# Channel-major products of a split-precision transformer block: a weight part times both halves of the input in one matmul

## The chip, the cores and the metric

The kernel runs on one core of a Trainium2 chip. The metric is the time of one execution on the device in microseconds (us), as the median over runs.

## What is computed

The reference takes 256 tokens of width 2048 through two blocks, in float32. The first has a mixer (a two-way state-space scan beside pooling), a gated convolutional network of width 5632 and a gated embedding. The second has attention with forgetting (16 heads of 128) and retention (8 heads). Nearly all of the work is in products of the 256 x 2048 activations, or wider ones, with large weight matrices:

```python
proj = hn @ w_in[i]                      # 2048 -> D_IN_PROJ, mixer
mix = concatenate([y_ssd, y_pool]) @ w_out[i]
up = hn @ w_up                           # 2048 -> 2 * 5632
... (gelu(conv(gate)) * val) @ w_down    # 5632 -> 2048
proj = einsum('bsd,de->bse', x, w_in)    # attention, retention
```

## The kernel before, in words

**Precision by parts.** Weights w and activations x are each held as a sum of two float32r parts, a high and a low one. A product is taken as `hi(w)*hi(x) + hi(w)*lo(x) + lo(w)*hi(x)`, so three matmuls stand for one.

**The stream of weights.** `Stream` (lines 84 to 172) loads pieces of 512 rows x 512 columns (1 MB) in the order of their use, up to four raw pieces ahead. `_split` (lines 105 to 125) makes the two parts of a piece: ScalarE (ACT) copies to `hi` (line 122), VectorE (DVE) subtracts to `lo` (line 123). `pump` (line 148) issues loads and splits when there are free slots; it is called at the start of each piece through `get` (line 162), and with `most=1` around the end of a unit. All engines run their instructions in the order in which the program gives them.

**Two kinds of units.** Each produces 512 output columns. `unit_a` (line 280) is token-major: two accumulators of 128 tokens x 512 columns (`pa`), activations as the stationary operand, 512 weight columns moving. `unit_b` (line 325) is channel-major: the weights are stationary, and the output has channels on the partitions and 256 tokens along the free axis (`pb`). It has four blocks j of 128 channels, two in each accumulator of [128, 2, 256], so two accumulators in all. Per k-tile q and block j it issues three matmuls of 256 columns (lines 339 to 341). There are 39 such units of 4 pieces with 4 k-tiles each: 6 in the mixer (B and C, x twice, the pooling input u, z twice), 21 in the gated network (a value and a gate unit in turn, the first value unit being token-major), 4 gates of attention, 8 query/key units of retention. That makes 39 x 4 x 4 x 4 = 2496 triples.

**Accumulators.** All PSUM tiles come from one pool with eight buffers of one bank each (line 180), whatever their use: `pa`, `pb`, and the small products of the work in between. A new tile takes a bank that is free; its first matmul waits until the former tile of that bank has been read for the last time.

**Work in between.** At the end of each piece `tick` (line 250) runs what `defer` put off, then the next `fillers`: the scan of the mixer by a hand-written list (`SCHED`, line 26), and the heads of attention. At a unit's end `unit_b` calls `pump(1)`, hands the first accumulator to the caller's function `evac(0, ...)`, ticks, and defers the second to the first tick of the next unit (lines 345 to 349). What `evac` does depends on the caller: the convolution of five taps in the mixer (`conv5`, line 623), pooling sums (`f_u`, line 645), the convolution of three taps, gelu and the product with the value (`eg`, line 975), silu times the attention output (line 1224), rotation (line 1278). The value units of the gated network keep their accumulators as they are until the gate unit after them has ended (lines 968 to 971).

**Temporaries.** Tiles of 512 floats per partition come from a pool of eight (`temp`, line 194). The transposed activations `xt[i]` are [128, 2, 4, 256]: part, k-tile, token (line 382).

Of the kernel before, what the change touches and what calls it, by code (L numbers as in the profile page):

```python
# [12 lines left out]
AF = mybir.ActivationFunctionType  # L13
# [3 lines left out]
P = 128  # L17
S = 256
D = 2048
# [3 lines left out]
MAXPAIR = 7  # L23
# (step of the state-space mixer, the weight piece after which it is put): D dt, B C B^T, A decays, X inputs, S masks,
# T states, Y outputs, G gates, Q sums of squares, N norms; the number is the pair of heads or the group
SCHED = [
# [6 lines left out]
OUT_ORDER = ((2, 0), (3, 0), (2, 1), (3, 1), (0, 0), (0, 1), (1, 0), (1, 1), (2, 2), (3, 2), (0, 2), (1, 2))  # L33
# the slots held by all but the weights while a piece is used: (how many pieces, slots)
LIVE = [
# [17 lines left out]
def constants():  # L53
    """Tables that depend on shapes alone."""
    i = np.arange(P)
    c1 = np.zeros((P, 1664), np.float32)
    c1[:, 0:128] = i[:, None] <= i[None, :]
    c1[:, 128:256] = i[:, None] >= i[None, :]
    c1[:, 256:384] = i[:, None] > i[None, :]
    c1[:, 384:512] = i[:, None] < i[None, :]  # L60
    c1[:, 512:640] = 1.0
    t = np.arange(S)
    for g, k in enumerate((2, 4, 8, 16)):
        cnt = np.clip(t + k - k // 2, 0, S) - np.clip(t - k // 2, 0, S)
        c1[:, 640 + g * S : 640 + (g + 1) * S] = np.float32(1.0) / cnt.astype(np.float32)
    ident = np.eye(P, dtype=np.float32)
    sel = np.zeros((P, 16), np.float32)
    for b in (0, 32, 64, 96):
        for h in range(16):
            sel[b + h, h] = 1.0  # L70
    mask = np.where(i[None, :] > i[:, None], np.float32(-1e30), np.float32(0.0)).astype(np.float32)
    c0 = np.concatenate([ident, mask, sel], axis=1)
    inv = np.float32(10000.0) ** (-np.arange(0, 256, 2, dtype=np.float32) / np.float32(256.0))
    ang = (np.arange(S, dtype=np.float32)[None, :] * inv.astype(np.float32)[:, None]).astype(np.float32)
    cs, sn = np.cos(ang), np.sin(ang)
    rope = np.concatenate([cs, cs, sn, sn], axis=1).astype(np.float32)
    lg = np.log1p(-np.exp2(-5.0 - np.arange(8, dtype=np.float64)))
    diff = t[None, :] - i[:, None]
    dec = np.where(diff[None] >= 0, np.exp(np.maximum(diff, 0)[None] * lg[:, None, None]) / 16.0, 0.0)
    decay = np.transpose(dec, (1, 0, 2)).reshape(P, 8 * S).astype(np.float32)  # L80
    return {"c_base": c0.astype(np.float32), "c_ssd": c1, "c_rope": rope, "c_decay": decay}


class Stream:
    """Weights in the order of their use: loaded ahead, each split in two float32r parts."""

# [40 lines left out]
    def fits(self, pairs, raws):  # L127
        """pairs, raws: how many are held; piece ndone is the first of the pairs"""
        d = self.ndone
        for t in range(d, d + max(pairs, 1) + 1):  # L130
            if self.live[t] + 2 * max(d + pairs - t, 0) + raws + (0 if t < d + pairs else 2) > NSLOT:
                return False
        return True

    def split_fine(self):
        """the first piece, k-tile by k-tile: yields after each"""
        key, parts, kt, n = self.order[0]
        r = self.raw.pop(0)
        hi = self.k.slot([P, kt, n], F32R, "hi")
        lo = self.k.slot([P, kt, n], F32R, "lo")  # L140
        self.pair[0] = (hi, lo)
        self.nsplit += 1
        for q in range(kt):
            self.k.nc.scalar.activation(hi[:, q], r[:, q], AF.Copy)
            self.k.nc.vector.tensor_sub(lo[:, q], r[:, q], hi[:, q].bitcast(F32))
            yield
# [28 lines left out]
class Kern:  # L175
# [9 lines left out]

# [1 line left out]
    def nm(self, s):  # L187
# [17 lines left out]

# [1 line left out]
    def mm(self, o, l, r, start, stop):  # L207
# [12 lines left out]
    def rstd(self, o, ssum, scale, eps):  # L220
        """1/sqrt(scale * ssum + eps)"""
        self.act(o, ssum, AF.Sqrt, scale=scale, bias=eps)
        self.nc.vector.reciprocal(o, o)
# [17 lines left out]

# [1 line left out]
    def fillers(self, fs, pieces):  # L243
# [20 lines left out]

# [1 line left out]
    def part_a(self, ps, toks, hi, lo, xs, n, first, last, mid=None):  # L266
        """token-major: ps[t] [128 tokens, n] += x^T' w"""
        kt = len(xs)
        for t in toks:
            o = ps[t][:, :n]  # L270
            c = slice(t * P, (t + 1) * P)
            for q in range(kt):
                self.mm(o, xs[q][0][:, c], hi[:, q, :n], first and q == 0, False)
                self.mm(o, xs[q][0][:, c], lo[:, q, :n], False, False)
            if mid:
                mid()
            for q in range(kt):
                self.mm(o, xs[q][1][:, c], hi[:, q, :n], False, last and q == kt - 1)

    def unit_a(self, keys, x, evac, n=512, phased=0, between=None, mid=None):  # L280
        """keys: the pieces; x(i): the k-tiles of piece i; the last `phased` pieces go token tile by token tile,
        with `between` between the two and `mid` shortly before the second's end"""
        W = self.W
        ps = [self.ps([P, 512], "pa") for _ in range(2)]
# [39 lines left out]
    def unit_b(self, keys, x, evac, nt=4):  # L324
        """channel-major: banks [128 channels, 2, 256 tokens] += w' x^T"""
        W = self.W
        ps = [self.ps([P, 2, S], "pb") for _ in range((nt + 1) // 2)]
        m = len(keys)
        for i in range(m):
            hi, lo = W.get(keys[i])  # L330
            xs = x(i)
            for q in range(len(xs)):
                xh, xl = xs[q]
                for j in range(nt):
                    o = ps[j // 2][:, j % 2]
                    c = slice(j * P, (j + 1) * P)
                    f = i == 0 and q == 0
                    e = i == m - 1 and q == len(xs) - 1
                    self.mm(o, hi[:, q, c], xh, f and j % 2 == 0, False)
                    self.mm(o, hi[:, q, c], xl, False, False)  # L340
                    self.mm(o, lo[:, q, c], xh, False, e)
            W.done()
            if i < m - 1:
                self.tick()
        W.pump(1)
        evac(0, ps[0])
        self.tick()
        self.defer(1, lambda: evac(1, ps[1]))
        W.pump(1)

    def rows_b(self, key, x, m):
        """few columns: [2 * 32, 256]: the high part's rows at 0, the low part's at 32"""
        W = self.W
        p = self.ps([P, 512], "pr")
        w, _ = W.get(key)
        for q in range(16):
            xh, xl = x(q // 4)[q % 4]
            self.mm(p[: 32 + m, :S], w[:, q, : 32 + m], xh, q == 0, False)
            self.mm(p[: 32 + m, :S], w[:, q, : 32 + m], xl, False, q == 15)
# [5 lines left out]

# [1 line left out]
    def new_t(self, name):  # L367
        return [None] * 4

    def xk(self, xt):  # L370
        return lambda i: [(xt[i][:, 0, q], xt[i][:, 1, q]) for q in range(4)]

    def to_t(self, src, xt, t, step=None):
        """the transpose of one token tile [128, 2048], in two parts"""
        for i in range(4):
# [16 lines left out]
    def evac_rms(self, y, ssq, g, u, t, p):  # L392
        """y = p * g and the sum of p squared"""
        c = slice(u * 512, (u + 1) * 512)
# [4 lines left out]
    def rms_add(self, h, y, ssq, t):  # L399
        """h += y * rstd, with the sums of squares of the new h"""  # L400
        r = self.tiny([P, 1], "r")
# [9 lines left out]
    def rms_apply(self, y, h, s2, g, t):  # L411
        """y = h * rstd * g"""
        r = self.tiny([P, 1], "r")
# [23 lines left out]

# [1 line left out]
    def plan(self):  # L439
# [75 lines left out]

# [1 line left out]
    def setup(self):  # L517
# [103 lines left out]

# [1 line left out]
    def conv5(self, dst, p, i0):  # L623
        """dst [128, 2, 256]: centred convolution of a bank p [128, 2, 256], then silu"""
        for j in range(2):
# [314 lines left out]

# [1 line left out]
    def ffn(self):  # L942
# [80 lines left out]

# [1 line left out]
    def ple(self):  # L1025
# [40 lines left out]

# [1 line left out]
    def fox(self):  # L1068
# [185 lines left out]

# [1 line left out]
    def ret(self):  # L1256
# [153 lines left out]
```

## Time and profile before

| | |
|---|---|
| runs | 2443.69, 2444.24, 2445.71 us; median 2444.24 |
| the profiled execution: span | 2444.1 us |
| TensorE (PE) busy | 99% of the span, 14504 matmuls |
| VectorE (DVE) busy | 57% |
| ScalarE (ACT) busy | 46% |
| granted TensorE clock | 0.994 of 2.4 GHz (mean) |
| DMA | 182 GB/s mean |

The profile gives no other time for the execution that it took than the span from its first to its last instruction; it stands 0.1 us from the median. Busy shares of PE are from modelled ends, so the distance between the starts of matmuls is the better measure of their cost. Lines with L208 are `mm`, L212 `tr`, L215 `act`, L218 `stt`: helpers that record each operation, so that the names of tiles tell the groups apart.

### The profile page before, as it was taken

The page shows a single profiled execution, that of the slowest core. Times are in us where ns is not written, and L with a number is a line of the kernel's source. Part 1 is how long each engine was busy: PE and PEld are TensorE (multiplying, and loading weights), DVE is VectorE, ACT ScalarE, POOL GpSimd, SP SyncE. Part 2 cuts the span into 40 slices and gives each one's busy share as a digit, 9 for nine tenths or more (in the row PEclk, how much of TensorE's full clock was granted, in tenths as well). Part 3 has the DMA queues.
Part 4 walks back from the last instruction along what each step waited for, and adds up shares of the span by engine and source line. Part 5 has one row for each costly group of instructions (what it writes and reads, how often), then busy time and mean ns, then how long its engine had stood idle before and what let it go on. Part 6 is the DMA issues. An engine that isn't in the chain of part 4 may idle for free.

```text
span 2444.1 us, 33532 instructions
## 1 busy us (share of the span) xinstructions
PE 2416.7 (99%) x14504; PEld 2150.1 (88%) x14504; DVE 1383.2 (57%) x1361; ACT 1123.1 (46%) x1245; POOL 0.9 (0%) x14
## 2 busy tenths in 40 slices
PE   9999999999999999999999999999999999999998
PEld 7999889999999888878888889988988888888886
DVE  6777475545545534466745455666655555556544
ACT  5467354434434433445646555643344334444331
POOL 0000000000000000000000000000000000000000
PEclk9999999999999999999999999999999999999999
DMA  8435554554554655555685576765455544546552
GB/s 316 139 121 203 210 213 150 190 174 154 189 173 156 224 173 197 198 210 193 201 170 167 130 162 154 189 238 192 166 191 169 173 160 168 175 160 233 208 190 86
DMA packets 239453, 444.00 MB, mean 182 GB/s; under 512 B 12095, under 2 KB 46793, under 8 KB 237769
## 3 DMA queue, kind: packets, MB, share of 16 engines
q1 hardware_dynamic: 239306, 441.87, 56.2%
q8 instruction: 113, 1.85, 0.3%
q14 instruction: 34, 0.28, 0.0%
HBM read 439.74 MB, written 2.10 MB: 181 GB/s over the span
## 4 chain that ended last, share of the span: by engine, by line
PE 96%; DVE 2%; ACT 1%; DMA 0%; issue 0%; SPq 0%; ACTq 0%; DVEq 0%
PE pa L208 53%; PE pb L208 36%; PE s L208 1%; PE o L208 1%; DVE lo L123 1%; PE y L208 1%; DVE h L218 0%; PE tp L212 0%; DMA raw<-in_w_in 0%; PE pl L208 0%; DVE xs L218 0%; PE pr L208 0%; PE qT L212 0%; PE yT L212 0%; PE pT L212 0%
## 5 line engine op out<-in xcount | busy, mean ns | idle before, releaser
L123 DVE TENSOR_TENSOR lo<-raw,hi 128x2048 fp32r<-128x2048 f32 x404 | 916.2, 2280 | 691.6 <-ACT hi L122 503.8
L122 ACT ACTIVATE hi<-raw 128x2048 fp32r<-128x2048 f32 x404 | 761.0, 1902 | 622.5 <-PE pa L208 278.5
L208 PE MATMUL pb<-xt,hi 128*128 128x256 f32 x4992 | 902.3, 283 | 0.0
L208 PEld LDWEIGHTS pb<-xt,hi 128*128 128x128 f32 x4992 | 778.8, 192 | 1.7 <-issue 0.5
L208 PE MATMUL pb<-xt,lo 128*128 128x256 f32 x2496 | 706.3, 283 | 0.0
L208 PE MATMUL pa<-hi,xt 128*128 128x512 f32 x2176 | 693.0, 394 | 5.5 <-ACT hi L122 2.2
L208 PEld LDWEIGHTS pa<-hi,xt 128*128 128x128 f32 x2176 | 411.0, 189 | 92.8 <-ACT hi L122 2.8
L208 PEld LDWEIGHTS pb<-xt,lo 128*128 128x128 f32 x2496 | 478.8, 192 | 0.0
L208 PE MATMUL pa<-lo,xt 128*128 128x512 f32 x1088 | 427.0, 392 | 5.3 <-DVE lo L123 4.4
L208 PE MATMUL pa<-hi,yt 128*128 128x512 f32 x1024 | 316.7, 390 | 0.0
L208 PEld LDWEIGHTS pa<-lo,xt 128*128 128x128 f32 x1088 | 205.5, 189 | 49.0 <-DVE lo L123 5.1
L208 PEld LDWEIGHTS pa<-hi,yt 128*128 128x128 f32 x1024 | 192.0, 188 | 39.7
L208 PE MATMUL pa<-hi,hid 128*128 128x512 f32 x704 | 218.8, 392 | 0.3 <-ACT hi L122 0.3
L208 PE MATMUL pa<-lo,yt 128*128 128x512 f32 x512 | 199.2, 389 | 0.0
L208 PEld LDWEIGHTS pa<-hi,hid 128*128 128x128 f32 x704 | 132.9, 189 | 28.4 <-ACT hi L122 0.7
L208 PE MATMUL pa<-lo,hid 128*128 128x512 f32 x352 | 137.6, 391 | 1.8 <-DVE lo L123 1.8
L208 PEld LDWEIGHTS pa<-lo,yt 128*128 128x128 f32 x512 | 96.1, 188 | 19.9
L208 PEld LDWEIGHTS pa<-lo,hid 128*128 128x128 f32 x352 | 66.3, 188 | 15.9 <-DVE lo L123 2.1
L215 ACT ACT_TABLE_LOAD x57 | 73.1, 1283 | 14.9 <-DVE sm L218 5.4
L215 ACT ACTIVATE junk<-pa 128x128 f32<-128x128 f32 (+1 forms) x80 | 26.2, 340 | 46.3 <-PE pa L208 46.3
L218 DVE SCALAR_TENSOR_TENSOR g<-pb,col,g 128x255 f32<-128x255 f32 x88 | 40.4, 480 | 10.3 <-ACT g L215 8.7
L215 ACT ACTIVATE g<-g 128x512 f32<-128x512 f32 x22 | 13.9, 631 | 59.0 <-DVE g L218 59.0
(236 smaller groups left out, 1116.4 us busy)
## 6 DMA issues: line engine op xcount, KB each, us to landing
raw<-in_w_ffn_up SPq DMA_DIRECT2D x88, 1024.0 KB
raw<-in_fox_w_in SPq DMA_DIRECT2D x64, 1024.0 KB
raw<-in_ret_w_in SPq DMA_DIRECT2D x64, 1024.0 KB
raw<-in_w_ffn_down SPq DMA_DIRECT2D x44, 1024.0 KB
raw<-in_ret_w_in SPq DMA_DIRECT2D x64, 512.0 KB
raw<-in_ret_w_out SPq DMA_DIRECT2D x32, 1024.0 KB
raw<-in_w_in SPq DMA_DIRECT2D x28, 1024.0 KB
raw<-in_w_out SPq DMA_DIRECT2D x16, 1024.0 KB
```

The costliest lines, as they stand in the source:

```text
L122: self.k.nc.scalar.activation(hi, r, AF.Copy)
L123: self.k.nc.vector.tensor_sub(lo, r, hi.bitcast(F32))
L208: self.nc.tensor.matmul(o, l, r, start=start, stop=stop, skip_group_check=True)
L215: self.nc.scalar.activation(o, i, f, **kw)
L218: self.nc.vector.scalar_tensor_tensor(o, x, s, y, op0=op0, op1=op1)
```

## The change

`unit_b` allocates four accumulators, one for each block j. The low weight part times the high half of x goes to columns 0 to 255 of it, as before with 256 columns. The high weight part is then multiplied with both halves of x in one matmul of 512 columns (the moving operand is two runs of 256 that lie 1024 floats apart), whose second half goes to columns 256 to 511. So hi*hi and lo*hi add up in the left half, hi*lo in the right. At the unit's end a new step adds the two: ACT copies the right half to a temporary, DVE adds the left half, for each of two blocks; `evac` then gets the temporary in place of the accumulator. The second pair is deferred as before. The callers are unchanged.

```diff
     def unit_b(self, keys, x, evac, nt=4):
         W = self.W
-        ps = [self.ps([P, 2, S], "pb") for _ in range((nt + 1) // 2)]
+        ps = [self.ps([P, 2, S], "pb") for _ in range(nt)]
...
-                xh, xl = xs[q]
+                xh, _, both = xs[q]
                 for j in range(nt):
-                    o = ps[j // 2][:, j % 2]
                     c = slice(j * P, (j + 1) * P)
                     f = i == 0 and q == 0
                     e = i == m - 1 and q == len(xs) - 1
-                    self.mm(o, hi[:, q, c], xh, f and j % 2 == 0, False)
-                    self.mm(o, hi[:, q, c], xl, False, False)
-                    self.mm(o, lo[:, q, c], xh, False, e)
+                    self.mm(ps[j][:, 0], lo[:, q, c], xh, f, False)
+                    self.mm(ps[j], hi[:, q, c], both, False, e)
...
         W.pump(1)
-        evac(0, ps[0])
+
+        def out(b):
+            t = self.temp([P, 2, S], "pbs")
+            for j in range(2):
+                o = ps[2 * b + j]
+                self.act(t[:, j], o[:, 1], AF.Copy)
+                self.nc.vector.tensor_add(t[:, j], o[:, 0], t[:, j])
+            evac(b, t)
+
+        out(0)
         self.tick()
-        self.defer(1, lambda: evac(1, ps[1]))
+        self.defer(1, lambda: out(1))
         W.pump(1)
...
     def xk(self, xt):
-        return lambda i: [(xt[i][:, 0, q], xt[i][:, 1, q]) for q in range(4)]
+        return lambda i: [(xt[i][:, 0, q], xt[i][:, 1, q], xt[i][:, :, q]) for q in range(4)]
```

Beyond this the diff takes the new third element of a k-tile apart in `rows_b` and removes comments.

## Rows read from the trace of the kernel before

**Rows 1.** The page: busy time by engine, then the chain by engine and by line

```profile
PE 2416.7 (99%) x14504; PEld 2150.1 (88%) x14504; DVE 1383.2 (57%) x1361; ACT 1123.1 (46%) x1245; POOL 0.9 (0%) x14
...
PE 96%; DVE 2%; ACT 1%; DMA 0%; issue 0%; SPq 0%; ACTq 0%; DVEq 0%
```

**Rows 2.** The chain in order of time: start us, us, what, how many

```profile
152.99 5.75 PE pb L208 x48
...
200.88 0.12 PE eo L208
...
352.65 477.37 PE pb L208 x3978
...
1576.14 5.87 PE pb L208 x49
...
1711.56 23.03 PE pb L208 x192
1734.59 10.91 PE pa L208 x48
```

**Rows 3.** Groups of matmuls: busy us, mean ns | idle before, releaser

```profile
L208 PE MATMUL pb<-xt,hi 128*128 128x256 f32 x4992 | 902.3, 283 | 0.0
L208 PE MATMUL pb<-xt,lo 128*128 128x256 f32 x2496 | 706.3, 283 | 0.0
```

**Rows 4.** Timeline, PE: 256 columns on stationary parts half as wide

```profile
70.94 3.80 PE L208 MATMUL pr<-xt,few 128*64 128x256 f32 x32
```

**Rows 5.** Groups by form on ACT and DVE: reads of a bank, 256 columns

```profile
L215 ACT ACTIVATE vo<-o 128x256 f32<-128x256 f32 x16 | 6.1, 380 | 28.0 <-PE o L208 28.0
...
L825 DVE TENSOR_TENSOR eo<-y,eo 128x256 f32<-128x256 f32 x8 | 3.3, 417 | 0.4 <-PE y L208 0.4
```

**Rows 6.** Busy time of PE, PEld, DVE, ACT, POOL in one stretch; clock, DMA

```profile
400.00:600.00 200.00, 200.00 (x1669) 200.00 (x1668) 100.12 (x81) 80.47 (x66) 0.00 (x0) 1.00 0.51 174
```

**Rows 7.** Timeline after the second x unit of the mixer: DVE, ACT, PE

```profile
128.33 2.29 DVE L123 TENSOR_TENSOR lo<-raw,hi 128x2048 fp32r<-128x2048 f32 x1 [1.58 <-PE pb L208]
130.54 3.97 DVE L218 SCALAR_TENSOR_TENSOR xs<-pb,col,xs 128x254 f32<-128x254 f32 x8
...
134.60 0.63 ACT L215 ACTIVATE xs<-xs 128x512 f32<-128x512 f32 x1 [7.47 <-DVE xs L218]
...
131.15 1.07 PE L212 MATMUL xt<-base,xs 128*128 128x128 f32 x8
```

**Rows 8.** Timeline after the unit of u: ACT

```profile
154.85 0.63 ACT L215 ACTIVATE mx<-us 128x512 fp32r<-128x512 f32 x1 [4.24 <-DVE us L666]
155.39 1.12 ACT L215 ACTIVATE e<-seg,acum 128x128 f32<-128x128 f32 x4
...
157.08 1.12 ACT L215 ACTIVATE e<-seg,acum 128x128 f32<-128x128 f32 x4
...
158.77 0.36 ACT L215 ACTIVATE eo<-eo 128x256 f32<-128x256 f32 x1
```

**Rows 9.** Timeline in the second z unit: DVE, ACT

```profile
198.07 4.49 DVE L123 TENSOR_TENSOR lo<-raw,hi 128x2048 fp32r<-128x2048 f32 x2 [1.32 <-ACT hi L122]
...
200.68 1.14 ACT L215 ACTIVATE e<-seg,acum 128x128 f32<-128x128 f32 x4 [0.35 <-PE seg L208]
```

**Rows 10.** Timeline, gated network: after its first gate unit (DVE), after its last (PE)

```profile
369.89 2.29 DVE L123 TENSOR_TENSOR lo<-raw,hi 128x2048 fp32r<-128x2048 f32 x1 [3.07 <-PE pb L208]
...
844.26 0.50 PE L208 MATMUL pa<-lo,hid 128*128 128x512 f32 x1 [1.83 <-DVE lo L123]
```

**Rows 11.** Timeline, attention: first gate unit's start (PE, DVE), third's end (DVE)

```profile
1492.64 0.49 PE L212 MATMUL pT<-base,w 128*128 128x128 f32 x3
1492.88 0.48 PE L208 MATMUL pb<-xt,hi 128*128 128x256 f32 x2
...
1496.02 0.69 DVE L1101 TENSOR_TENSOR junk<-pa,sq 128x512 f32<-128x512 f32 x1
...
1577.35 2.29 DVE L123 TENSOR_TENSOR lo<-raw,hi 128x2048 fp32r<-128x2048 f32 x1 [3.08 <-ACT hi L122]
```

More of the change, by code (lines that the diff above doesn't have):

```diff
@@ L356, in rows_b @@
         for q in range(16):
-            xh, xl = x(q // 4)[q % 4]
+            xh, xl, _ = x(q // 4)[q % 4]
             self.mm(p[: 32 + m, :S], w[:, q, : 32 + m], xh, q == 0, False)
```

## The prediction

> **What bounds the kernel now.** I read the page's busy times first: PE 99%, the others 57% and less; then the chain that ended last: 96% of the span is PE's [rows 1]. PE's busy time is from modelled ends, so I took the price of a matmul from the chain in order of time, where pieces of PE work follow each other with nothing between: start to start, not duration. Channel-major matmuls of 256 columns: 3978 in 477.37 us, 192 in 23.03 us, both 120.0 ns. Token-major ones of 512 columns: 48 in 10.91 us, 227.3 ns [rows 2]. (The 283 ns of the groups [rows 3] is the modelled duration, of which the rest overlaps.) The reader is to see that twice the columns cost not twice but 1.89 times as much: some 12.7 ns belong to the instruction and not to its columns. And PE waits for almost nothing: the `pb` groups show 0.0 us of idle time before them [rows 3]. What saves PE time saves time, and any new wait of PE is paid in full.
>
> **Part 1, fewer matmuls.** There are 4992 + 2496 = 7488 matmuls in the units, 2496 triples [rows 3]. A triple costs 3 x 120.0 = 360.0 ns. The new pair is 256 + 512 columns: 120.0 + 227.3 = 347.3 ns. Saved: 12.7 ns x 2496 = 31.7 us. The columns that move stay the same; only the price of 2496 instructions, each with a weight load, goes. No row shows a 512-column moving operand in two runs, nor these two widths in turn. From below: the two runs cost what two matmuls of 256 do, and nothing is saved. From above: the third matmul's fixed part might also shrink the neighbour's; with stationary parts half as wide, 256 columns come at (3.80 - 0.28) / 31 = 113.5 ns [rows 4], which would give some 6 ns more per pair, 16 us. I take 31.7, since the 512-column row is the same operation on the same banks, and its moving operand alone differs.
>
> Weighed against a page: the Trainium skill, TensorE: Matmul & The Clock Gate, Back-to-back issue gap, gives a matmul alone N / 2.4 + 2.5 ns at full clock. By it the third matmul's fixed part would be 2.5 ns, the saving 6 us. The rows say 12.7 (120.0 and 227.3 ns, granted clock 1.00 [rows 6]), so here the trace speaks for the change and the skill's page against it.
>
> **Part 2, the halves added.** Four copies and four additions per unit, 39 units: 156 copies x 380 ns = 59 us on ACT, 156 additions x 417 ns = 65 us on DVE, by the nearest reads of a bank with 256 columns [rows 5]. In the unit-after-unit stretch DVE is busy 100 of 200 us, ACT 80 [rows 6]; they have room, and I cost the work itself at nothing. Its cover is the next unit, 4 x 16 x 347 ns = 22 us. If that cover goes, a unit pays its two additions in a row, 0.8 us, 33 us in all. Reading the temporary in place of the bank changes no price that I can see. The order lo before hi asks for `lo` two matmuls, 0.24 us, earlier: 156 pieces x 0.24 = 37 us if every `lo` came at the last moment, nothing if none does. The groups show no idle time before `pb` [rows 3], so I take nothing.
>
> **Part 3, two more banks per unit.** This is where I expect the loss. Of eight banks a unit now holds four, and its second pair until the next unit's first tick. A unit that follows another with nothing between finds the other four free: no wait in most of the gated network (20 of its 21 units) and in retention, where token-major units with two banks stand between. Where small products are put in between, PE gets to a matmul whose bank has not been read out. The trace shows no bank numbers; I take it that a tile gets the bank that is free first, and read the release from the last reader's row.
>
> - x to u: u holds four, the second x unit the other four. The first pair is added behind the split that DVE ends at 130.62, the second behind the eight convolution steps (134.51), the silu (135.2) and two copies; with 0.8 us for the new additions the third bank is free at about 136.9. PE wants it for `xt` at 131.15 [rows 7]: 5.7 us.
> - u to z: five small tiles are open when z starts at 152.99 [rows 2]. z finds one bank; the others come when ACT has read `seg` (156.5, 158.2) and `eo` (159.1), all behind the `mx` that waits for DVE [rows 8]. With 0.35 us of work on each block between: 3.2 + 1.3 + 0.6 = 5.1 us.
> - z, second unit, first tick: two banks for three tiles, since the former pair waits for DVE's splits until 202.6. The third comes when ACT has read the first `seg`, about 202.6 with two copies ahead [rows 9]; PE is there at 200.9 [rows 2]: 1.7 us.
> - First value unit of the gated network: two `val` banks are held. The third block waits for DVE, which ends a split at 372.2 and adds until 372.6, against 370.6: 2.1 us with the fourth. The stall of 1.83 us at 844.26 grows by the additions and copies ahead of that split, 1.5 us [rows 10].
> - Attention, first gate: two `pa`, two `qT`, one `pT` are unread, three banks are free. The fourth block wants its bank at 1492.88 + 1.04 = 1493.9; the first `pa` is read at 1496.71: 2.8 us. Third to fourth gate: the split on DVE ends at 1579.64, the addition at 1580.1, against 1576.14 + 1.04 [rows 2, 11]: 2.9 us if no small tile comes free before; I take half, 1.5.
>
> Sum of the waits: 5.7 + 5.1 + 1.7 + 2.1 + 1.5 + 2.8 + 1.5 = 20.4 us. From below 0 us, if ACT and DVE get to the banks in another order or a wait makes the next one vanish; from above about 40, since ten seams have small tiles between (six in the mixer, one in the gated network, three in attention) and the worst read costs 4 us or so.
>
> **Sum.** 2444.1 - 31.7 + 20.4 = 2432.8 us, against the profiled execution's span, which stands 0.1 us from the median of the runs.
>
> **The rivals.**
> 1. The banks come free in time. For it: waits that I count one after the other may swallow each other, since while PE waits ACT and DVE catch up. Against: at the first two seams the last readers stand behind chains that go to and fro between DVE and ACT (idle 7.47 and 4.24 us for each other [rows 7, 8]), and no wait of PE shortens those. With 0 to 8 us of waits: 2412 to 2420 us.
> 2. Slower, by the banks: the small tiles of the mixer and of attention have four banks or two instead of six or four, everywhere and not at seven places. This decides from 31.7 us of waits up. At 40 us: 2452 us. Temporaries add to it: one per pair more from a pool of eight, and an ACT copy that waits for one holds up the splits behind it.
> 3. The 512-column matmul does not do what it says: two runs cost as two matmuls of 256, nothing is saved, and the waits stay: 2444.1 + 20.4 = 2464 us. Against it: the 227.3 ns of one run of 512 [rows 2]. The Trainium skill's formula of part 1 would end near it, at 2444.1 - 6 + 20.4 = 2458 us, an estimate. No row bears that formula out, so it has a small share of this rival's chance.
>
> **How the numbers follow.** A measurement of this kernel can tell about 0.2%, 4.9 us, from no change. Chances: my forecast, 10 to 29 us of waits, 0.52; rival 1 0.20; rival 2 0.15; rival 3 0.13. Most of the forecast (waits under 26.8 us) and all of rival 1 are faster by over 0.2%: 0.44 + 0.20 = 0.64. Its upper end and the near part of rival 2, 0.08 + 0.07, are within: 0.15. The rest, 0.21, is slower. The likeliest time is 2433; its own range is 2422 to 2441. The range to hold 8 in 10 reaches to 2416 (part of rival 1, or a little more saved) and to 2453 (rival 2), and leaves out most of rival 3.
>
> **What would show it.** Right: `pb` in 4992 matmuls, pieces of 32 in 5.56 us; ACT and DVE up by about 59 and 65 us; idle time before `xt`, `pb` or `eo` with releaser ACT or DVE near 130, 155 and 1494 us, about 20 us in all. Wrong in part 1: a piece of 32 in 5.76 us. Wrong in part 3: idle time of PE unchanged (rival 1), or pieces of waiting spread over the small products of mixer and attention (rival 2).

## The result and the profile after

The changed kernel takes 2460.74 us (four runs, 2453.39 to 2464.45), the kernel before 2443.97 in the same session: ratio 1.0066, 95% interval 1.0048 to 1.0083. It is slower, by about 17 us; the prediction had 2433 us, at most 2453, and the other sign. The profiled execution took 2459.21 us, with a span of 2457.4. (In every run the time stands 1.7 to 2.8 us above the span. So the span of 2444.1 of the kernel before belongs to an execution some 2 us longer than the median, and that the two numbers stand 0.1 us apart is chance. Below, spans are held against spans.)

The page of the kernel after, its line of busy times, its chain by engine, and the groups of `pb` and of the additions:

```profile
PE 2406.1 (98%) x12008; PEld 2018.6 (82%) x12008; DVE 1440.4 (59%) x1517; ACT 1177.4 (48%) x1401; POOL 1.0 (0%) x14
...
PE 88%; DVE 4%; ACT 2%; issue 1%; DMA 1%; ACTq 0%; DVEq 0%; SPq 0%
...
L208 PE MATMUL pb<-xt,hi 128*128 128x512 f32 x2496 | 885.9, 399 | 0.0
L208 PE MATMUL pb<-xt,lo 128*128 128x256 f32 x2496 | 706.5, 283 | 12.5 <-DVE pbs L351 5.0
...
L215 ACT ACTIVATE pbs<-pb 128x256 f32<-128x256 f32 x156 | 53.8, 380 | 71.0 <-PE pb L208 69.5
...
L351 DVE TENSOR_TENSOR pbs<-pb,pbs 128x256 f32<-128x256 f32 x156 | 58.7, 420 | 26.0 <-ACT pbs L215 26.0
```

The reader is to see three things. The change does what it says: 2496 matmuls fewer, 2496 of 512 columns. PE's modelled busy time falls by 10.6 us only. And PE, which was 96% of the chain [rows 1], is 88%: the low-part matmuls, without any idle time ahead of them before [rows 3], now have 12.5 us, and the releaser named is the new addition.

Where PE waited, by the view of waits after (what waits, for what: us in total, times, longest). None of these rows is in the same view of before:

```profile
PE pb L208 <- DVE pbs L351: 5.0, 2, 3.1
PE pb L208 <- ACT e L215: 4.5, 2, 3.8
...
PE xt L212 <- DVE pbs L351: 2.9, 1, 2.9
PE pb L208 <- ACT qk L215: 2.7, 1, 2.7
...
PE eo L208 <- DVE pbs L351: 2.2, 1, 2.2
...
PE cb L208 <- DVE pbs L351: 1.2, 1, 1.2
```

The price of a pair, from the chain in order of time (start, us, what, how many), first two pieces of 32, then a stretch of the gated network, then three units of retention:

```profile
182.17 5.55 PE pb L208 x32
...
360.58 5.65 PE pb L208 x32
...
386.29 361.15 PE pb L208 x2043
...
1728.75 22.61 PE pb L208 x128
...
1776.71 22.19 PE pb L208 x128
...
1846.97 22.61 PE pb L208 x128
```

Two matmuls cost 361.15 / 2043 x 2 = 353.6 ns, 22.61 / 64 = 353.3 in one unit and 22.19 / 64 = 346.7 in another: two levels, and only the lower is the forecast (347.3). Over all undisturbed pairs the mean distance from start to start is 116.94 + 235.43 = 352.37 ns. So the pairs saved (360.0 - 352.37) x 2496 = 19.0 us, not 31.7.

The other term I get by adding up, over the whole trace, what each distance between starts on PE exceeds the median of its kind (tile and columns), where by over 60 ns: 48.9 us before, 79.5 after. So stalls grew by 30.6 us, not 20.4. Together: 2444.1 - 19.0 + 30.6 = 2455.7, against a span of 2457.4. I use the same sum for each experiment below that leaves nothing out; it comes within 2.5 us of the profiled span each time.

**How one seam looks.** The timeline of after where the second x unit ends and u begins (start, us, engine, operation, [idle before <- releaser]), to be held against [rows 7]:

```profile
127.08 0.75 DVE L351 TENSOR_TENSOR pbs<-pb,pbs 128x256 f32<-128x256 f32 x2
...
128.16 3.99 DVE L218 SCALAR_TENSOR_TENSOR xs<-pbs,col,xs 128x254 f32<-128x254 f32 x8 [0.34 <-ACT xs L215]
...
132.25 0.63 ACT L215 ACTIVATE xs<-xs 128x512 f32<-128x512 f32 x1 [3.63 <-DVE xs L218]
132.78 0.64 ACT L215 ACTIVATE pbs<-pb 128x256 f32<-128x256 f32 x2
133.18 0.76 DVE L351 TENSOR_TENSOR pbs<-pb,pbs 128x256 f32<-128x256 f32 x2 [1.03 <-ACT pbs L215]
...
133.66 1.97 PE L212 MATMUL xt<-base,xs 128*128 128x128 f32 x8 [2.90 <-DVE pbs L351]
```

The first two additions free a bank each, then the convolution of the first pair runs: eight steps on DVE, the silu on ACT. Only then does ACT copy the second pair, and DVE adds. The transposes `xt` wait for the first of these two additions. The second pair's sums were finished for over 6 us; nothing but the order on two queues kept the banks.

And the clock. Windows of the kernel after behind this stall and behind the one of attention (busy us by engine, then granted clock, DMA share, GB/s):

```profile
135.00:139.00 4.00, 4.00 (x15) 3.52 (x15) 3.10 (x7) 0.63 (x2) 0.00 (x0) 0.50 0.00 0
139.00:143.00 4.00, 4.00 (x23) 3.44 (x22) 1.63 (x4) 2.33 (x6) 0.00 (x0) 0.94 0.00 0
1509.00:1512.00 3.00, 3.00 (x11) 2.56 (x12) 1.81 (x4) 1.48 (x10) 0.00 (x0) 0.55 0.81 254
```

After PE had stood still for 2.9 us the granted clock was 0.50, the lower of its two levels, and until about 139 us a pair took 640 ns (427 + 213) in place of 353. By those excesses the tail, the time lost to the lower clock once PE runs again, cost about 1.9 us here, 2.3 behind the stall at 157 and 1.4 behind the one at 1506. There was none behind stalls of 2.0 us at 384, 2.3 at 213 and 3.3 at 1591. The length of the stall does not tell these apart. A stall of only 1.5 us at 1245 was followed by a granted clock of 0.50 from 1249 to 1252 us; and in the profiled execution of the reverse kernel below, the stalls that answer to those at 213 and 1591 do have a tail (0.50 from 217 to 220 and from 1600 to 1606 us).

### The profile page after: what moved, and what is told of

The parts are those of the page before. It is cut to its first block, busy times and chain, and to the rows that moved or that the text cites. A ratio compares the mean times of both kernels' runs of the same rounds, so it can differ in the third digit from the quotient of the medians.

```text
span 2457.4 us, 28854 instructions
## 1 busy us (share of the span) xinstructions
PE 2406.1 (98%) x12008; PEld 2018.6 (82%) x12008; DVE 1440.4 (59%) x1517; ACT 1177.4 (48%) x1401; POOL 1.0 (0%) x14
## 4 chain that ended last, share of the span: by engine, by line
PE 88%; DVE 4%; ACT 2%; issue 1%; DMA 1%; ACTq 0%; DVEq 0%; SPq 0%
PE pa L208 51%; PE pb L208 31%; PE s L208 1%; DVE lo L123 1%; PE o L208 1%; DMA raw<-in_fox_w_in 1%; PE y L208 1%; ACT hi L122 1%; DVE h L218 0%; DVE g L218 0%; PE tp L212 0%; PE pl L208 0%; ACT g L215 0%; PE yT L212 0%; ACT e L215 0%
## 5 line engine op out<-in xcount | busy, mean ns | idle before, releaser
L208 PE MATMUL pb<-xt,hi 128*128 128x512 f32 x2496 | 885.9, 399 | 0.0
L208 PE MATMUL pb<-xt,lo 128*128 128x256 f32 x2496 | 706.5, 283 | 12.5 <-DVE pbs L351 5.0
L208 PEld LDWEIGHTS pb<-xt,hi 128*128 128x128 f32 x2496 | 471.4, 189 | 114.2 <-issue 0.2
L215 ACT ACTIVATE pbs<-pb 128x256 f32<-128x256 f32 x156 | 53.8, 380 | 71.0 <-PE pb L208 69.5
L351 DVE TENSOR_TENSOR pbs<-pb,pbs 128x256 f32<-128x256 f32 x156 | 58.7, 420 | 26.0 <-ACT pbs L215 26.0
L218 DVE SCALAR_TENSOR_TENSOR g<-pbs,col,g 128x255 f32<-128x255 f32 x88 | 40.7, 483 | 9.0 <-ACT g L215 7.4
```

What stands on the lines that cost most here:

```text
L208: self.nc.tensor.matmul(o, l, r, start=start, stop=stop, skip_group_check=True)
L215: self.nc.scalar.activation(o, i, f, **kw)
L218: self.nc.vector.scalar_tensor_tensor(o, x, s, y, op0=op0, op1=op1)
L351: self.nc.vector.tensor_add(t[:, j], o[:, 0], t[:, j])
```

## The experiments

### Where the loss is: banks without pairs, units apart

**Three matmuls again, but four accumulators, copies and additions.**

```diff
-                    self.mm(ps[j], hi[:, q, c], both, False, e)
+                    self.mm(ps[j][:, 0], hi[:, q, c], xh, False, False)
+                    self.mm(ps[j][:, 1], hi[:, q, c], xl, False, e)
```

> Three matmuls of 256 columns as before the change, but in four banks, with the copies and additions: the price of part 2 and part 3 alone. Theory W (waits for banks cost some 32 us, the clock's fall after them included): before plus 30 to 34 us, 2474 to 2478 us, with PE's waits for the additions at the same seams of the mixer, the gated network and attention. Rival (the waits come from faster matmuls that outrun ACT and DVE): before plus 10 us at most.

Measured: 2474.11 us, ratio 1.0120 (1.0105 to 1.0135). With the old price of matmuls the banks, copies and additions alone cost 29.3 us: theory W's time, and just under its 30 to 34; the rival had 10 at most. The stalls in its trace, taken in its shortest run, are 24.0 us more than before. Against this kernel the pairs give back 2474.1 - 2460.7 = 13.4 us. That is less than 19.0, since the stalls of after are 6.6 us more than those here (3.6 of them are a wait for loads, told below).

**The new product in the gated network and retention alone.** The units of the mixer and the gates of attention call the old `unit_b`, kept as `unit_b2`.

```diff
-        self.unit_b(self.keys("w_in", 2048), x, ...
+        self.unit_b2(self.keys("w_in", 2048), x, ...
```

> The new product in the gated network and in retention alone (29 units), the old one with two banks in the mixer and in attention (10 units). Theory W: waits of some 4 us are left (first value unit, first down pieces), the saving is 29 x 64 x 6.7 = 12 us at 353 ns per pair: 8 us less than before, 2436 us; 20 us less if pairs cost 347 ns. Rival (the loss is spread over all units, by ACT and DVE work or by copies that hold up splits): no better than before, 2444 us or more.

Measured: 2437.82 us (nine runs), ratio 0.9963 (0.9950 to 0.9976): faster than both, near theory W's 2436 and not the rival's 2444 or more. But the nine lie in two clusters, three at 2428.7 to 2430.8 and six at 2436.2 to 2440.6. In the profiled one, of the upper cluster, the pairs of all but two units are at 353 ns (mean 352.9).

**The reverse: the new product in the mixer and attention alone.**

> The reverse: the new product in the mixer and in the four gates of attention alone (10 units, 640 pairs), the old one with two accumulators in the gated network and in retention. Theory W (the loss is waits for accumulators where small products stand between the units): 640 pairs save 4 to 8 us, waits cost about 28 us; 20 to 24 us slower than the kernel before, 2465 to 2469 us. Rival (the loss is spread over all units, by the copies, the additions or the pairs' price): a quarter of the units, a quarter of the loss; within 5 us of the kernel before.

Measured: 2469.48 us, ratio 1.0104 (1.0090 to 1.0118), half a microsecond above theory W's range and far from the rival's. Ten units of 39 carry the whole loss: stalls 78.2 us, 29.3 more than before, and (360.0 - 350.9) x 640 = 5.8 us saved. Its view of waits has the rows of after, nearly to the tenth:

```profile
PE pb L208 <- ACT e L215: 4.8, 2, 3.8
PE pb L208 <- DVE pbs L351: 3.1, 1, 3.1
PE pb L208 <- ACT qk L215: 2.7, 1, 2.7
PE xt L212 <- DVE pbs L351: 2.7, 1, 2.7
...
PE eo L208 <- DVE pbs L351: 2.2, 1, 2.2
```

### What the waits are made of: freeing all four at once

**Both additions of both pairs first, then the splits and the caller's function.**

```diff
-        W.pump(1)
...
-            evac(b, t)
+            return t
-        out(0)
+        t0, t1 = out(0), out(1)
+        W.pump(1)
+        evac(0, t0)
         self.tick()
-        self.defer(1, lambda: out(1))
+        self.defer(1, lambda: evac(1, t1))
```

> The changed kernel with the release of all four accumulators at once when a unit ends: both copies and both additions of both pairs stand ahead of the splits of the unit's end and ahead of the caller's function; that function then reads the temporaries as before. Theory C (PE waits because the additions that free an accumulator stand in line behind splits and behind the caller's chains between DVE and ACT): the third accumulator is free some 1 us after the unit's last matmul, and most of the 30 us of waits at the seams goes, 15 to 25 us less than the changed kernel; about 2436 to 2446 us. Rival B (four accumulators plus the small products' are simply too many for eight, whatever the release): the waits stay within 5 us of what they are, 2455 to 2464 us. Rival D (the splits, now behind the additions, come late): new waits for low or high parts, slower than 2464 us.

Measured: 2438.61 us (seven runs, 2436.40 to 2439.49), ratio 0.9972 (0.9961 to 0.9982): 22 us less than the change as it was, and now faster than before. Theory C's range of times held. The same seam in the timeline of this kernel:

```profile
125.71 1.41 DVE L350 TENSOR_TENSOR pbs<-pb,pbs 128x256 f32<-128x256 f32 x4
...
127.15 2.29 DVE L123 TENSOR_TENSOR lo<-raw,hi 128x2048 fp32r<-128x2048 f32 x1
...
129.36 3.99 DVE L218 SCALAR_TENSOR_TENSOR xs<-pbs,col,xs 128x254 f32<-128x254 f32 x8
...
130.07 1.07 PE L212 MATMUL xt<-base,xs 128*128 128x128 f32 x8
```

Four additions in a row, 1.41 us, are over at 127.12; the convolution still ends at 133.35, and `xt` waits for nothing. What remains, in its view of waits:

```profile
PE pb L208 <- ACT e L215: 3.2, 1, 3.2
PE pb L208 <- DVE pbs L350: 2.8, 1, 2.8
...
PE pb L208 <- ACT qk L215: 2.7, 1, 2.7
...
PE pb L208 <- DVE lo L123: 1.1, 2, 0.7
```

The first and the third row end with ACT's reads of small products (`e`, `qk`), which no order of the additions frees sooner: for these places rival B stands, that four accumulators and the small products are too many for eight banks in this order of work. The second row, between the third and the fourth gate of attention, is as long as it was (3.1 us in after). The last row is rival D, small: two splits came late. And theory C's reason covers only half of what was gained. In the profiled executions the span fell by 19.7 us. The stalls are 68.7 us, 10.8 below after's 79.5, where I had 15 to 25. Another (352.37 - 349.26) x 2496 = 7.8 us are the pairs, which stood at 347 ns through most of the gated network:

```profile
358.64 370.60 PE pb L208 x2138
```

370.60 / 2138 x 2 = 346.7 ns. All seven runs lie within 3.1 us; the four of the change as it was lay within 11.1.

**Both together: new product in the gated network and retention alone, freed at once.**

> The new product in the gated network and retention alone, with all four accumulators released at once at the unit's end. By theory C the remaining waits of the gated network, 3 to 4 us, shrink to about 1: 2 to 3 us less than without this (2438 us median, clusters near 2430 and 2438), so near 2428 or 2436 us by the pairs' level. By rival B no difference. By rival D, splits come late by 1 us in some units: up to 10 us slower than without.

Measured: 2427.78 us (2425.81 to 2428.64), ratio 0.9928 (0.9915 to 0.9942), the best of all. Its stalls are 49.2 us, those of before. Its gated network is at 347 ns but for the last three units, retention at 353 but for one, in the mean 349.0, so 2444.1 + 0.3 - (360.0 - 349.0) x 1856 = 2424.0; span 2424.0:

```profile
351.48 370.60 PE pb L208 x2138
```

370.60 / 2138 x 2 = 346.7 ns. Of the 10 us to the kernel without early release, then, most is the level of the pairs: (352.9 - 349.0) x 1856 = 7.2 us between the two profiled executions, and 5.7 us are stalls. That kernel's lower cluster, 2428.7 to 2430.8, comes within 3 us of this one. None of the five runs here lies in an upper cluster; whether early release is what keeps them out of it is not shown.

### The price of a pair

**The halves of x side by side, so that the operand is one run of 512.**

```diff
-                xt[i] = self.slot([P, 2, 4, S], F32R, "xt")
+                xt[i] = self.slot([P, 4, 2, S], F32R, "xt").rearrange("p q a s -> p a q s")
```

> The halves of each k-tile of x lie next to each other, so the 512-column moving operand is one run. Theory R (a moving operand in two runs costs some 6 ns more): the hi matmul falls from 236 to about 230 ns, a pair from 353 to 347 ns, 2496 x 6 = 15 us less than the changed kernel, about 2446 us. Rival P (the 6 ns belong to the turn of 256 and 512 columns, or to a phase that the engine keeps): pairs stay at 353 ns in most units and the time at 2460 us.

Measured: 2459.10 us, ratio 1.0058 (1.0038 to 1.0078); pairs at 352.1 ns on average, as after. The two runs of the operand are not what costs. The same within the kernel that has the new product in two stages:

> As the run before with x's halves in one run of 512. Theory R: pairs at 347 ns, 29 x 64 x 12.7 = 24 us saved less 4 us of waits: 2424 us. Rival P: as without it, 2436 us.

Measured: 2433.44 us (eight runs, 2428.02 to 2440.24), ratio 0.9958 (0.9943 to 0.9972). Its interval overlaps that of the kernel without the edit (0.9950 to 0.9976), and its runs again lie in two clusters. In its profiled execution the gated network is at 347 ns and most of retention at 353: both levels within one execution.

**High part first.**

```diff
-                    self.mm(ps[j][:, 0], lo[:, q, c], xh, f, False)
-                    self.mm(ps[j], hi[:, q, c], both, False, e)
+                    self.mm(ps[j], hi[:, q, c], both, f, False)
+                    self.mm(ps[j][:, 0], lo[:, q, c], xh, False, e)
```

> The changed kernel with the two matmuls of a pair in the other order: the 512 columns on the high part first, then the 256 on the low part. Theory O (the price of the 512-column matmul depends on what stands ahead of it, a 256-column one with its own weight load): order inside the pair changes nothing in a long row of pairs, since they alternate in either order; 353 or 347 ns per pair start to start, time as the changed kernel, 2453 to 2464 us. Theory L (the low part, wanted first, is what is late): the low part is wanted 0.23 us later, so single stalls at the starts of pieces shrink; 1 to 5 us less than the changed kernel and pairs at 347 ns.

Measured: 2458.65 us (2455.46 to 2464.30), ratio 1.0063 (1.0048 to 1.0079). Theory O's range, and theory L's too, which had 1 to 5 us less than after. Theory L's reason fails: the stalls are 85.6 us, 6.1 more than after's. The level that it named is there, in most of the gated network:

```profile
388.90 354.46 PE pb L208 x2043
```

354.46 / 2043 x 2 = 347.0 ns, and 349.1 as the mean of all pairs. But both levels come in either order, and this is one execution: that the order decides the level is not shown, nor that it does not.

**A matmul of this form alone.** The low part's matmuls are left out, and with them that third of every channel-major product.

```diff
-                    self.mm(ps[j][:, 0], lo[:, q, c], xh, f, False)
-                    self.mm(ps[j], hi[:, q, c], both, False, e)
+                    self.mm(ps[j], hi[:, q, c], both, f, e)
```

> The changed kernel without the low weight part times the high half of x (that third of the products is left out, its weight parts are still made): per k-tile and block one matmul of 512 columns on the high part, each after one of its own width. Theory A (it is the turn of widths that costs): 227 ns start to start, as in the token-major units of the kernel before. Theory M (a matmul of this form, stationary weights and both halves of x moving, costs more by itself): 230 to 236 ns. The time tells little, some 2155 to 2190 us, as the loads of weights may come to bound it; the price is read in a unit where PE does not wait.

Measured: 2217.16 us in one run, above the range that I gave: PE waits more for splits (`hi`, 16.7 us) and for additions (some 32 us) than I thought. The price is read in a unit of retention, from its chain:

```profile
1654.02 14.51 PE pb L208 x64
```

14.51 / 64 = 226.7 ns. So two runs, the same bank, both halves moving: all at the price of [rows 2], as long as matmuls of one width follow each other. That is theory A's price.

**Four and four.**

```diff
                 for j in range(nt):
...
-                    self.mm(ps[j][:, 0], lo[:, q, c], xh, f, False)
-                    self.mm(ps[j], hi[:, q, c], both, False, e)
+                    self.mm(ps[j][:, 0], lo[:, q, cs[j]], xh, f, False)
+                for j in range(nt):
+                    self.mm(ps[j], hi[:, q, cs[j]], both, False, e)
```

> The changed kernel with the matmuls of a k-tile grouped by width: four of 256 columns on the low part, then four of 512 on the high part. Theory A (the turn of 256 and 512 columns makes the 512-column one dear, 236 ns in place of 227 to 230): most matmuls now follow one of their own width, so 4 x 120.0 + 4 x 227.3 = 1389 ns per k-tile, 347.3 per pair everywhere, no second level; 2496 x 5 ns = 13 us less than the changed kernel at its slower level, about 2446 to 2450 us. Theory P (the level is set by how a stretch of matmuls starts, not by the turn of widths): both levels, 346 to 347 and 353 ns per pair, show again, and the time stays between 2450 and 2464 us.

Measured: 2461.58 us (2460.11 to 2462.27), ratio 1.0070 (1.0056 to 1.0083), in theory P's range of times, but not with its two levels. The chain has one level in retention where after has two:

```profile
1732.59 22.45 PE pb L208 x128
...
1780.39 22.43 PE pb L208 x128
```

22.45 / 64 = 350.8 ns. The runs lie within 2.2 us. Neither theory had that. Turning between the widths twice per k-tile in place of eight times took away the two levels of this kernel, but not the cost; the four 512-column matmuls of a k-tile are followed after 235, 235, 232 and 228 ns on average. And the same in the gated network and retention alone:

> The new product in the gated network and retention alone, with the matmuls of a k-tile grouped by width. Theory A: 1856 pairs at 347.3 ns in place of 1856 triples at 360.0 save 23.6 us, waits in the gated network cost 3 to 4 us; about 2425 us in all runs, without a second cluster. Theory P: as the ungrouped kernel of this kind, runs in two clusters near 2430 and 2438 us.

Measured: 2436.06 us (2431.29 to 2437.48), ratio 0.9963 (0.9951 to 0.9976); pairs at 350.8 ns in the profiled run. Theory A's 2425 us is missed by 11. One run lies near 2431, four near 2436: that grouping by four takes the levels away in every execution is not shown.

**Sixteen and sixteen, with early release.**

```diff
             for q in range(len(xs)):
-                xh, _, both = xs[q]
                 for j in range(nt):
...
+                    self.mm(ps[j][:, 0], lo[:, q, cs[j]], xs[q][0], i == 0 and q == 0, False)
+            for q in range(len(xs)):
+                for j in range(nt):
                     e = i == m - 1 and q == len(xs) - 1
...
+                    self.mm(ps[j], hi[:, q, cs[j]], xs[q][2], False, e)
```

> The changed kernel with early release of all four accumulators (2438.6 us) and with the matmuls of a whole piece grouped by width: sixteen of 256 columns, then sixteen of 512. Theory A (each turn of width costs some 7 ns: grouping by four showed 1403 ns per k-tile where 4 x 120.0 + 4 x 227.3 = 1389): two turns in a piece, 16 x 347.3 + 14 = 5571 ns, 348.2 per pair in every stretch; against a mix of 347 and 353 in the kernel with early release, 2 to 6 us less, 2433 to 2437 us, and no two levels. Theory P (a level of its own, which grouping by four averaged): 351 per pair again, 2438 to 2441 us. The low parts are now wanted 1.9 us sooner as a whole: if a split is late, waits for lo show at the starts of pieces, up to 1 us each.

The chain of this kernel, in the gated network and in two units of retention:

```profile
373.79 355.83 PE pb L208 x2043
...
1709.20 22.27 PE pb L208 x128
...
1756.79 22.26 PE pb L208 x128
```

355.83 / 2043 x 2 = 348.3 ns, 22.27 / 64 = 348.0 ns, where theory A had 348.2 and theory P 351. The levels are gone in this execution. Start by start: after each turn to 512 columns the first five stand 233, 236, 228, 233 and 231 ns apart, then it is 227 to the end; after the turn back the first are 113 and 119 ns, then 120. So the first five of a piece cost 26 ns more than five at 227, and the two after the turn back 8 less. (That alternating widths never settle to 227 is a reading of these rows, not a cause that a run shows.) The time, however, is 2438.62 us (2436.61 to 2439.48), ratio 0.9974 (0.9964 to 0.9985): the same as without grouping, since that kernel had 346.7 in most of the gated network, below what grouping gives, and 353 in most of retention, above it. I had expected 2 to 6 us less. The same for the best kernel:

> The new product in the gated network and retention alone, early release, pieces grouped by width. Theory A: 1856 pairs at 348.2 ns; the kernel without grouping has 347 in the gated network and 353 in retention, so (1344 x 1.2 - 512 x 5) = 1 us less to no difference: 2425 to 2428 us, pairs at 348 in retention. Theory P: 351 everywhere, 1344 x 4 - 512 x 2 = 4 us more, 2432 us.

Measured: 2428.65 us, ratio 0.9935 (0.9922 to 0.9949), pairs at 347.8 ns: no difference from 2427.78; theory A had the price and missed the time by 0.65 us. And the best kernel with adjacent halves:

> The best kernel so far (new product in the gated network and retention alone, accumulators released at once, 2427.8 us) with the two halves of x side by side, so that the moving operand is one run of 512. If the operand's form plays no part, as the earlier run with it says, the same time within 5 us, 2424 to 2432 us, moved only by the pairs' level; if it helps where no seam disturbs, all 1856 pairs at 346 to 347 ns, 5 us less than at 353 in retention: 2422 to 2425 us.

Measured: 2428.42 us, ratio 0.9934 (0.9921 to 0.9948): no difference either.

## Why the prediction was wrong

**Part 1, fewer matmuls: the saving per triple was mis-sized.** The step was "I take 31.7, since the 512-column row is the same operation on the same banks, and its moving operand alone differs". That is true of the matmul alone (226.7 ns when it follows its like), but the bound that I named in the same paragraph, that no row shows "these two widths in turn", was where it failed. In turn, a pair costs 347 or 353 ns and stays at one of them for hundreds of matmuls; the mean of after was 352.4. The term measured 19.0 us: 12.7 us short. The sign that I had named gave both answers: pieces of 32 in 5.55 us, the 5.56 that would be right, and elsewhere in 5.65, half way to the 5.76 that would be wrong. By the formula of the Trainium skill, TensorE: Matmul & The Clock Gate, Back-to-back issue gap, the saving would have been some 6 us, an estimate; the 19.0 measured agree neither with it nor with the 31.7 of the rows.

**Part 2, the halves added: right in the main.** ACT is up by 54 us and DVE by 57, against 59 and 65 forecast, with 380 and 420 ns for each read of a bank, as [rows 5] had it; the gated network, where unit follows unit, has no stall above 0.35 us but at its ends. So the work itself costs next to nothing. The earlier `lo`, taken at nothing, cost two waits in the gated network, 0.7 us in all. The place of the additions in the queues, however, belongs to part 3: setting them first took 10.8 us off the stalls.

**Part 3, two more banks: right in kind, too small.** At the seams that were listed, the excess of after less that of before in the same stretch, half-clock tails included:

| seam | forecast | measured |
|---|---|---|
| x to u | 5.7 | 5.7 |
| u to z | 5.1 | 6.2 |
| z, second unit | 1.7 | 2.2 |
| first value unit | 2.1 | 2.2 |
| first stall of the down product | 1.5 | 0.7 |
| attention, first gate | 2.8 | 4.2 |
| third to fourth gate | 1.5 | 3.4 |
| sum | 20.4 | 24.6 |

Two steps failed. "I take half, 1.5" for third to fourth gate: no small tile came free in time, and the whole 2.9 was paid and more. And the half clock behind a stall was no term, though it cost about 5.6 us at three places; from x to u the 5.7 is right by luck, as the waits themselves were shorter than forecast (2.9 us at `xt` and 0.6 at `ac`) and a tail filled the sum up. The list was also not complete: small waits at `dtT`, `cb`, `xt`, `seg`, `eo` and at two places of the gated network (those for `lo`) make 4.2 us, for the most part of the kind that rival 2 spread over the mixer.

Near 1233 to 1252 us attention's small products lost 3.6 us more, tail included, and this is no matter of banks. The stall before `c` stands in every kernel that has the new product in the gated network with nothing left out, also in the best one, whose attention is the old one (1.1 us). It stands in none without, not in the one with three matmuls in four accumulators. The timeline shows why, first before, then after:

```profile
1225.43 0.19 DVE L1125 TENSOR_TENSOR v<-fT,bf 128x32 f32<-128x32 f32 x1 [3.70 <-PE fT L212]
```

```profile
1237.74 1.92 ACT L122 ACTIVATE hi<-raw 128x2048 fp32r<-128x2048 f32 x1 [3.97 <-DMA raw<-in_fox_w_in]
1239.69 2.29 DVE L123 TENSOR_TENSOR lo<-raw,hi 128x2048 fp32r<-128x2048 f32 x1 [3.86 <-ACT hi L122]
1241.90 0.18 DVE L1133 TENSOR_TENSOR v<-fT,bf 128x32 f32<-128x32 f32 x1
...
1246.74 0.81 PE L208 MATMUL c<-tri,sp 128*16 128x128 f32 x6 [1.49 <-issue]
```

Before, DVE begins the steps from `fT` to `c` when PE has made `fT`; after, they stand behind a split whose weights landed late. ACT's splits wait 21.8 us for loads of these weights after, and no such wait is in the view of before. Why the loads come later there no run shows. The rest, to 30.6, are stalls that differ without a pattern, the largest 1.8 us less at the start.

**The sum and the rivals.** With stalls alone mis-sized the result would have been 2444.1 - 31.7 + 30.6 = 2443, no change; with the pairs alone, 2444.1 - 19.0 + 20.4 = 2445.5, no change. The sign came from both at once. I had priced each rival with the other term at its best value: rival 2 kept the 31.7 us, rival 3 kept the 20.4. What happened was nearly rival 2's waits (30.6 us of stalls, not all for banks) with two fifths of rival 3's shortfall (12.7 of 31.7 us), and no case held that. The range ended where rival 2 did.

**What stays open.** What sets the level of 347 or 353 ns in a stretch. It changes at stalls, differs between executions of one kernel and goes with the spread of the runs as far as the profiles tell. With early release the profiled executions are at 347 in most of the gated network, and grouping by pieces gives one price in between; but no run shows the cause. Open too is why the loads of attention's first weights come later where the gated network has the new product.

## What to carry to other kernels

When a change doubles the accumulators that a stage holds, look first at what frees them: put the reads that free a bank ahead of everything else that the stage's end has for those engines, and let the long functions work on the copy. Use the costlier scheme only in stages where unit follows unit; here both together turned a loss of 0.7% into a gain of the same size, the second alone into one of 0.4%. And price an instruction from a row in which its neighbours are those that it will have.

## What the hardware showed that was not expected

- A 512-column matmul costs 226.7 ns after its like, and 228 to 236 in the first five places behind 256-column ones. In strict turn a pair has two stable prices, 346.7 and 353.3 ns, in one execution. The lower is near the 347.3 of the prediction, but made of other terms: 117 + 230 ns in the gated network with early release, not 120.0 + 227.3.
- A stall of PE costs more than itself where the granted clock falls to 0.50: 1.4 to 2.3 us of tail behind three stalls of 2.8 to 5 us, and none behind another of 3.3, whose counterpart in another kernel's execution had one. The Trainium skill, TensorE: Matmul & The Clock Gate, A second HAM failure mode: psum-queue depth-cycling, tells of a kernel that cycles through PSUM banks, whose PE idles for short times, often, between groups of matmuls, and whose clock goes back and forth between half and full. The windows of after show the same two levels (0.50, and 0.94 once it rises), but behind single stalls.
